# Two-layer diffusion backbone: in each attention unit, the foreign piece behind the scores, then the turn, then the values

## Chip, core and metric

The kernel runs on one core of a Trainium2 chip. The metric is the device time of one execution in microseconds (us), the median of several runs. Five engines work side by side, each through its own queue of instructions in a fixed order: PE (TensorE, matrix products and transposes), DVE (VectorE), ACT (ScalarE), POOL (GpSimd) and SP (SyncE, which here only issues DMAs). PEld is the load of a product's stationary operand, which overlaps PE.

## What is computed

The reference is a backbone of two layers on 128 context tokens and 512 latent tokens, width 1024, in float32. The layer the change touches is the second, attention with 8 query heads and 2 key heads of 128 channels:

```
def blocked_attention(q, k, v):
    ...
    def one_block(qi):
        s = jnp.einsum('bqkgd,bskd->bkgqs', qi, k, ...) * sm_scale
        p = jax.nn.softmax(s, axis=-1).astype(v.dtype)
        return jnp.einsum('bkgqs,bskd->bqkgd', p, v)
...
y = blocked_attention(q, k, v) @ w_o[i]
x = x + g1 * y
```

Latent queries attend to 128 cached and 512 own keys (640 in all), context queries to the 128 context keys. A projection to q, k and v goes before, an output projection behind, and a SwiGLU feed-forward block follows in each layer.

## The kernel before

Every float32 operand of a product is held as two rounded parts, h (high) and l (low), and each product is done three times (h by h, l by h, h by l; the table THREE). The helper `pair` makes the parts: ACT copies the source to h (line 146), a second engine subtracts h from the source to give l (line 147). That engine is DVE, except for the split of weight tiles within the attention loop, where `ws.eng = G` gives it to POOL.

The attention loop runs over 34 units: 32 latent units, named by head and query block (0_0, 0_1, ... 7_3), and two context units, c0 and c1. A unit has these steps:

- `scores`: 6 products into the PSUM tile s_0_0 and so on (3 pairs of 128x320). There is one buffer for it (`ps_tile(..., 0)`), so the next scores wait until this unit's exponentials are read out of it.
- `peak` on DVE (maximum, line 1331, and its scaling, line 1332), `exps` on ACT (line 1338), `weights` (reciprocal, line 1348, then the normalising of pe: on ACT at line 1240 for even query blocks, on DVE at line 1238 for odd ones).
- `turn`: 5 transposes of pe on PE into the one buffer of tile t (`ps_tile(..., 1)`, line 1354). `keep`: `pair` from t to pt_0h and pt_0l, ACT then DVE. The next turn needs that buffer free.
- `values`: for each two query blocks, 15 products (line 1371) from pt into the tile o; `store`: `pair` from o to the attention output, ah and al.

Between them PE is given pieces of other work through `fills`: first `pq`, the q projection of heads 3 to 7 (8 pieces of 6 products each per head, tiles pq_7 to pq_11), then `wa`, the first half of the output projection (4 pieces of 6 products for each of 8 column blocks, wa_0 to wa_7). All of these share the third buffer (`ps_tile(..., 2)`). When a block's last piece is done, its tile is read out: a q head by `scaled` (DVE line 538, ACT lines 543 and 1184), then squares, rotary terms and `pair`; an output block by `residual`, two DVE instructions (lines 513 and 527). Only then may the next block's first product write that buffer. Behind the loop follow the second half of the output projection (wb) and the feed-forward block.

How many pieces go into a unit is decided by the counters `spent` and `work`. A scheduler then fixes the order of each engine's queue from the written order and from its own view of what is ready, so that steps of one unit may stand among those of the next.

Of the kernel before, what the change touches and what calls it, by code (L numbers as in the profile page):

```python
# [62 lines left out]
def hybrid_step(  # L63
# [707 lines left out]
    with tc.tile_pool(name="pool1", bufs=1) as p1:  # L771
# [317 lines left out]
        with tc.tile_pool(name="pool4", bufs=1) as p4:  # L1089
# [11 lines left out]
                last=last0,  # L1101
# [7 lines left out]
    with tc.tile_pool(name="pool2", bufs=1) as p2:  # L1109
# [274 lines left out]
        units = []  # L1384
# [30 lines left out]
        with ExitStack():  # L1415
            for u, unit in enumerate(units):
                pipe.now += 1
                for f in posts:
                    f()
                posts = []  # L1420
                unit.scores()
                last = units[u - 2] if u > 1 and units[u - 2].values else None
                if last:
                    last.values()
                if u:
                    units[u - 1].turn()
                unit.peak()
                unit.exps()
                if u:
                    units[u - 1].keep()  # L1430
                unit.weights()
                spent += W_UNIT + (W_VALUES if last else 0)
                while fills and not posts and spent + W_PIECE / 2 <= work * (u + 1) / len(units):
                    posts = [f for f in (fills.pop(0)(),) if f]
                    spent += W_PIECE
                if last:
                    last.store()
                pipe.run_due()
# [38 lines left out]
    def last1(kn):  # L1477
# [60 lines left out]
        last=last1,  # L1538
# [116 lines left out]
```

## Time and profile before

| what | value |
|---|---|
| median of 3 runs | 1357.52 us (1357.14 to 1358.26) |
| the profiled execution | 1356.08 us, its span 1354.3 us |
| mean granted TensorE clock | 0.993 |
| PE busy | 1326.0 us, 98% of the span |
| DVE, ACT, POOL busy | 1068.6, 637.7, 46.3 us |
| attention loop, first scores to the first product of wb | 709.85 to 867.95 us |

A line of a timeline gives the start, the duration, the engine, the source line, the operation, the tile written and those read, and in brackets how long the engine stood idle before and what ended it. In such lines buffer and unit numbers are left out: `t<-kc,pe` is a turn, whichever unit's. PE starts the next product while the last still drains, so the distance between starts is what a product costs PE; ends lie somewhat later.

### The profile page before, as it was taken

The numbers are of one execution on the slowest core, as the hardware profiler recorded it, in microseconds if no ns is written. First come the engines' busy times: TensorE is split into PE (matmuls) and PEld (weight loads), VectorE is DVE, ScalarE is ACT, GpSimd is POOL, SyncE is SP. The second block draws the span as 40 slices with busy tenths as digits, with TensorE's granted clock in tenths as the row PEclk, the third lists the DMA queues.
The fourth block names the chain that finished last, engine by engine and source line by source line (L and its number), as shares of the span: only waits on it lengthen the run. The fifth ranks groups of instructions, "written<-read, shape, count | busy, mean of one in ns | idle before, by whom it ended". The sixth has DMA issues, their size and how long they took to land.

```text
span 1354.3 us, 22409 instructions
## 1 busy us (share of the span) xinstructions
PE 1326.0 (98%) x8952; PEld 1295.1 (96%) x8952; DVE 1068.6 (79%) x2025; ACT 637.7 (47%) x1159; POOL 46.3 (3%) x56
## 2 busy tenths in 40 slices
PE   8999999999999999999999999999999999999996
PEld 6899999999999999999998999999999999999995
DVE  4899897978999999899877677589876777446744
ACT  5433246753145522454666675477541355314543
POOL 0000000000000000000022221000000000000001
PEclk9999999999999999999999999999999999999998
DMA  9735522125543454334331110131134022311212
GB/s 365 286 125 171 171 94 94 63 67 176 179 141 109 146 187 151 120 137 164 133 101 48 48 48 32 51 137 60 38 137 171 32 94 76 112 63 63 78 47 78
DMA packets 36807, 155.53 MB, mean 115 GB/s; under 512 B 3936, under 2 KB 11104, under 8 KB 25952
## 3 DMA queue, kind: packets, MB, share of 16 engines
q1 hardware_dynamic: 36704, 154.12, 33.0%
q8 instruction: 70, 1.15, 0.4%
q14 instruction: 33, 0.27, 0.1%
HBM read 148.60 MB, written 2.88 MB: 112 GB/s over the span
## 4 chain that ended last, share of the span: by engine, by line
PE 82%; DVE 12%; ACT 3%; issue 2%; DMA 1%; SPq 0%; POOL 0%; DVEq 0%; ACTq 0%; POOLq 0%
PE fi L648 28%; PE fo L294 18%; PE fi L294 8%; PE pi L294 6%; PE pq L294 5%; PE po L294 4%; DVE junk L377 4%; PE wb L294 2%; PE wa L294 2%; PE o L1371 2%; PE s L1321 2%; DVE wl_fi_p L147 1%; PE t L1354 1%; DMA rawa<-wada 1%; DMA x<-xT 1%
## 5 line engine op out<-in xcount | busy, mean ns | idle before, releaser
L146 ACT ACTIVATE wh_fi_p<-raw_fi 128x512 fp32r<-128x512 f32 x252 | 154.5, 627 | 226.0 <-PE fi L648 122.3
L377 DVE CUSTOM_DVE_ANT_0 junk<-rawa,silb 128x512 f32<-128x512 f32 (+1 forms) x280 | 224.0, 800 | 7.9 <-DMA rawa<-wada 3.5
L147 DVE TENSOR_TENSOR wl_fi_p<-raw_fi,wh_fi_p 128x512 fp32r<-128x512 f32 x252 | 171.3, 687 | 65.6 <-ACT wh_fi_p L146 65.3
L146 ACT ACTIVATE wh_fo<-raw_fo 128x1024 fp32r<-128x1024 f32 (+1 forms) x48 | 47.5, 990 | 147.8 <-PE fo L294 129.5
L648 PE MATMUL fi<-bh,wl_fi_p 128*128 128x320 f32 x288 | 89.0, 309 | 0.0
L648 PE MATMUL fi<-bh,wh_fi_p 128*128 128x320 f32 x288 | 88.8, 308 | 0.0
L648 PE MATMUL fi<-ah,wl_fi_p 128*128 128x320 f32 x288 | 88.7, 308 | 0.0
L648 PE MATMUL fi<-al,wh_fi_p 128*128 128x320 f32 x288 | 88.7, 308 | 0.0
L648 PE MATMUL fi<-ah,wh_fi_p 128*128 128x320 f32 x288 | 88.4, 307 | 0.0
L648 PE MATMUL fi<-bl,wh_fi_p 128*128 128x320 f32 x288 | 88.4, 307 | 0.0
L294 PE MATMUL fo<-al,wh_fo 128*128 128x384 f32 (+1 forms) x352 | 81.0, 311 | 0.0
L294 PE MATMUL fo<-ah,wh_fo 128*128 128x384 f32 x352 | 80.8, 311 | 0.1
L294 PE MATMUL fo<-ah,wl_fo 128*128 128x384 f32 x352 | 80.5, 310 | 0.0
L294 PE MATMUL fo<-bh,wh_fo 128*128 128x384 f32 x328 | 75.2, 310 | 0.0
L294 PE MATMUL fo<-bh,wl_fo 128*128 128x384 f32 (+1 forms) x328 | 75.1, 310 | 0.0
L294 PE MATMUL fo<-bl,wh_fo 128*128 128x384 f32 x328 | 75.0, 310 | 0.0
L513 DVE SCALAR_TENSOR_TENSOR x<-fo,mod,x 128x128 f32<-128x128 f32 (+1 forms) x52 | 18.5, 359 | 70.7 <-PE fo L294 67.2
L648 PE MATMUL fi<-x0h,wh_fi_p 128*128 128x320 f32 x216 | 68.1, 319 | 0.5
L648 PE MATMUL fi<-xh,wh_fi_p 128*128 128x320 f32 x216 | 67.9, 320 | 0.5 <-ACT fi L660 0.4
L648 PE MATMUL fi<-xl,wh_fi_p 128*128 128x320 f32 x216 | 66.5, 309 | 0.0
L648 PE MATMUL fi<-xh,wl_fi_p 128*128 128x320 f32 x216 | 66.5, 309 | 0.0
L648 PE MATMUL fi<-x0h,wl_fi_p 128*128 128x320 f32 x216 | 66.4, 308 | 0.0
(376 smaller groups left out, 3774.7 us busy)
## 6 DMA issues: line engine op xcount, KB each, us to landing
raw_fi<-wfi SPq DMA_DIRECT2D x44, 1024.0 KB, 4.8
rawa<-wada SPq DMA_DIRECT2D x84, 512.0 KB, 3.4
raw_fo<-wfo SPq DMA_DIRECT2D x16, 1024.0 KB, 4.9
raw_ada<-wada SPq DMA_DIRECT2D x12, 512.0 KB, 7.3
raw_in<-win SPq DMA_DIRECT2D x6, 1024.0 KB, 5.2
raw_fo<-wfo SPq DMA_DIRECT2D x8, 768.0 KB, 4.3
raw_qkv<-wqkv SPq DMA_DIRECT2D x6, 1024.0 KB, 5.5
raw_out<-wout SPq DMA_DIRECT2D x4, 1024.0 KB, 5.9
```

Of the source, the lines that this page charges most:

```text
L146: S.activation(h, src, AF.Copy)
L147: eng.tensor_tensor(out=l, in0=src, in1=h.bitcast(F32), op=ALU.subtract)
L294: PE.matmul(ps[:, h, 0 : hi - lo], w[a][:, k, cols], rhs[b][:, k0 + k, lo:hi], start=k == 0 and a == b, stop=k == kn - 1 and a == 1,)
L377: op = V.tensor_tensor_reduce(out=self.junk, in0=raw[:, cols], in1=self.silb[:, c, cols], scale=1.0, scalar=0.0, op0=ALU.mult, op1=ALU.add ...
L513: V.scalar_tensor_tensor(out=xs, in0=got[:, 0 : b - a], scalar=mod[l][:, gate0 + m, c : c + 1], in1=xs, op0=ALU.mult, op1=ALU.add,)
L648: PE.matmul(out, w[a][:, k, :], ops.get(OPERAND[p], b)[:, k, :], start=fresh and k == 0 and a == b, stop=k == ops.kn - 1 and a == 1, skip_ ...
L1321: PE.matmul(self.ps[:, hf, 0:HT], bufB[a][:, self.h, q0 : q0 + P], kt[b][:, self.kv, hf * HT : hf * HT + HT], start=n == 0, stop=n == 2,)
L1354: PE.transpose(flat(pt)[:, s * P : s * P + P], self.pe[:, s * P : s * P + P], ident)
L1371: PE.matmul(po[:, 0 : 2 * P], vt[a][:, self.kv, s * P : s * P + P], got[b][:, s, :], start=s == 0 and n == 0, stop=s == 4 and n == 2,)
```

## The change

Within a unit, the written order was scores, values of the unit before last, turn of the last unit, peak, exponentials, keep, weights, pieces, store. It becomes scores, peak, exponentials, pieces, turn and keep of the last unit, values, weights, store. Nothing is added or left out. PE, DVE and ACT run the same instructions in another order within the attention loop; the orders of POOL and of SP's DMAs stay as they were.

```
--- before.py
+++ after.py
@@ -1420,19 +1420,18 @@
                 posts = []
                 unit.scores()
                 last = units[u - 2] if u > 1 and units[u - 2].values else None
-                if last:
-                    last.values()
-                if u:
-                    units[u - 1].turn()
                 unit.peak()
                 unit.exps()
-                if u:
-                    units[u - 1].keep()
-                unit.weights()
                 spent += W_UNIT + (W_VALUES if last else 0)
                 while fills and not posts and spent + W_PIECE / 2 <= work * (u + 1) / len(units):
                     posts = [f for f in (fills.pop(0)(),) if f]
                     spent += W_PIECE
+                if u:
+                    units[u - 1].turn()
+                    units[u - 1].keep()
+                if last:
+                    last.values()
+                unit.weights()
                 if last:
                     last.store()
                 pipe.run_due()
```

Three places show what the scheduler makes of it. Names carry the unit here.

First place, PE queue between the output blocks wa_2 and wa_3 (from the sixth head on). Before, the last two rows of wa_2 and what follows, up to the first rows of wa_3:

```order
L294 MATMUL wa_2_8414<-ah_68,wl_wo0_1_8192 128x384
L294 MATMUL wa_2_8414<-ah_68,wl_wo0_1_8192 128x256
L1321 MATMUL s_5_3_8466<-kth_6548,ah_68 128x320 x2
L1321 MATMUL s_5_3_8466<-ktl_6549,ah_68 128x320 x2
L1321 MATMUL s_5_3_8466<-kth_6548,al_69 128x320 x2
L1371 MATMUL o_5_1_8473<-pt_5_0h_8404,vth_6552 128x256
L1371 MATMUL o_5_1_8473<-pt_5_0l_8405,vth_6552 128x256
...
L1371 MATMUL o_5_1_8473<-pt_5_0h_8404,vtl_6553 128x256
L1354 MATMUL t_5_2_8489<-kc_73,pe_5_2_8445 128x128 x5
L294 MATMUL wa_3_8507<-ah_68,wh_wo0_1_8191 128x384
L294 MATMUL wa_3_8507<-ah_68,wh_wo0_1_8191 128x256
```

Now:

```order
L294 MATMUL wa_2_8386<-ah_68,wl_wo0_1_8164 128x384
L294 MATMUL wa_2_8386<-ah_68,wl_wo0_1_8164 128x256
L1354 MATMUL t_5_1_8454<-kc_73,pe_5_1_8379 128x128 x5
L294 MATMUL wa_3_8479<-ah_68,wh_wo0_1_8163 128x384
L294 MATMUL wa_3_8479<-ah_68,wh_wo0_1_8163 128x256
L1321 MATMUL s_5_3_8466<-kth_6548,ah_68 128x320 x2
L1321 MATMUL s_5_3_8466<-ktl_6549,ah_68 128x320 x2
L1321 MATMUL s_5_3_8466<-kth_6548,al_69 128x320 x2
```

Before, scores (s_5_3), 15 products of values (o_5_1) and a turn (t_5_2) lay between the end of wa_2 and the start of wa_3. Now only a turn (t_5_1) does. The same holds from wa_1 to wa_2, wa_3 to wa_4 and wa_4 to wa_5.

The same place in DVE's queue, before:

```order
L1331 TENSOR_REDUCE mx_5_2_8442<-s_5_2_8429 128x1
L1332 TENSOR_SCALAR mx_5_2_8442<-mx_5_2_8442,rq_6554 128x1
L147 TENSOR_TENSOR pt_5_0l_8405<-t_5_1_8436,pt_5_0h_8404 128x5x128
L1348 RECIPROCAL su_5_2_8446<-su_5_2_8446 128x1
L513 SCALAR_TENSOR_TENSOR x_67<-wa_2_8414,mod1_78,x_67 128x128
L527 SCALAR_TENSOR_TENSOR x_67<-wa_2_8414,mod1_78,x_67 128x512
L1331 TENSOR_REDUCE mx_5_3_8495<-s_5_3_8466 128x1
L1332 TENSOR_SCALAR mx_5_3_8495<-mx_5_3_8495,rq_6554 128x1
```

Now:

```order
L1331 TENSOR_REDUCE mx_5_2_8436<-s_5_2_8429 128x1
L513 SCALAR_TENSOR_TENSOR x_67<-wa_2_8386,mod1_78,x_67 128x128
L1332 TENSOR_SCALAR mx_5_2_8436<-mx_5_2_8436,rq_6554 128x1
L527 SCALAR_TENSOR_TENSOR x_67<-wa_2_8386,mod1_78,x_67 128x512
L1348 RECIPROCAL su_5_2_8440<-su_5_2_8440 128x1
L147 TENSOR_TENSOR pt_5_0l_8406<-t_5_1_8454,pt_5_0h_8405 128x5x128
L1331 TENSOR_REDUCE mx_5_3_8473<-s_5_3_8466 128x1
L1332 TENSOR_SCALAR mx_5_3_8473<-mx_5_3_8473,rq_6554 128x1
```

The two read-outs of wa_2 (lines 513 and 527) moved ahead of the keep of t_5_1, and the first of them stands between the maximum of unit 5_2 and its scaling.

Second place, PE queue about the turn of unit 1_1 (the pq phase), before:

```order
L294 MATMUL pq_8_7352<-bh_70,wh_qkv4_0_7181 128x322
L1354 MATMUL t_1_1_7497<-kc_73,pe_1_1_7468 128x128 x5
L294 MATMUL pq_8_7352<-bl_71,wh_qkv4_0_7181 128x320
L294 MATMUL pq_8_7352<-bl_71,wh_qkv4_0_7181 128x322
L294 MATMUL pq_8_7352<-bh_70,wl_qkv4_0_7182 128x320
L294 MATMUL pq_8_7352<-bh_70,wl_qkv4_0_7182 128x322
L1371 MATMUL o_1_1_7531<-pt_1_0h_7471,vth_6552 128x256
L1371 MATMUL o_1_1_7531<-pt_1_0l_7472,vth_6552 128x256
L1371 MATMUL o_1_1_7531<-pt_1_0h_7471,vtl_6553 128x256
```

Now:

```order
L294 MATMUL pq_8_7324<-bh_70,wl_qkv4_0_7180 128x322
L1354 MATMUL t_1_1_7509<-kc_73,pe_1_1_7446 128x128 x5
L1371 MATMUL o_1_1_7570<-pt_1_0h_7461,vth_6552 128x256
L1371 MATMUL o_1_1_7570<-pt_1_0l_7462,vth_6552 128x256
L1321 MATMUL s_1_3_7524<-kth_6548,ah_68 128x320 x2
L1321 MATMUL s_1_3_7524<-ktl_6549,ah_68 128x320 x2
L1321 MATMUL s_1_3_7524<-kth_6548,al_69 128x320 x2
L1371 MATMUL o_1_1_7570<-pt_1_0h_7461,vtl_6553 128x256
L294 MATMUL pq_9_7541<-bh_70,wh_qkv4_1_7318 128x320
```

Before, four products of pq_8 stood behind the turn, and eight of the values ahead of the scores s_1_3. Now the first values stand directly behind the turn, and the scores behind the second of them. The same shape stands at the turns of 0_1 (seven values, then the scores), 2_1 and 3_3.

Third place, ACT's queue about the turns of head 0, before:

```order
L146 ACTIVATE pt_0_0h_7241<-t_0_0_7229 128x5x128
L1338 ACTIVATE pe_0_1_7238,su_0_1_7239<-s_0_1_7222,mx_0_1_7235,rq_6554 128x640
L146 ACTIVATE pt_0_0h_7241<-t_0_1_7272 128x5x128
L146 ACTIVATE wh_qkv5_0_7565<-raw_qkv5_6912 128x1024
L146 ACTIVATE ah_68<-q_2_7152 128x640
L1338 ACTIVATE pe_0_2_7281,su_0_2_7282<-s_0_2_7265,mx_0_2_7278,rq_6554 128x640
```

Now:

```order
L1338 ACTIVATE pe_0_1_7232,su_0_1_7233<-s_0_1_7222,mx_0_1_7229,rq_6554 128x640
L146 ACTIVATE pt_0_0h_7259<-t_0_0_7253 128x5x128
L146 ACTIVATE wh_qkv5_0_7537<-raw_qkv5_6912 128x1024
L146 ACTIVATE pt_0_0h_7259<-t_0_1_7290 128x5x128
L146 ACTIVATE ah_68<-q_2_7152 128x640
L1338 ACTIVATE pe_0_2_7275,su_0_2_7276<-s_0_2_7265,mx_0_2_7272,rq_6554 128x640
```

The split of a weight tile (wh_qkv5_0), whose second half POOL does, stood behind the copy of t_0_1 and stands ahead of it now. On DVE, as before, the rotary sum of head 2 and the scaling of unit 0_2's maximum stand ahead of the subtraction for t_0_1.

## The prediction

> **What bounds the kernel now.** The first section of the page gives the bound, and the table of stretches the place. The stretches run from the scores of 0_1 (716.84) over those of 1_1, 2_1, 3_0 and 4_3 and those of 7_0 to the first product of wb (867.95).
>
> ```profile
> PE 1326.0 (98%) x8952; PEld 1295.1 (96%) x8952; DVE 1068.6 (79%) x2025; ACT 637.7 (47%) x1159; POOL 46.3 (3%) x56
> ...
> core 0: us, PE busy (x) PEld busy (x) DVE busy (x) ACT busy (x) POOL busy (x), PEclk, DMA share, GB/s
> ...
> 716.84:736.42 19.58, 17.89 (x122) 16.51 (x123) 13.71 (x27) 12.70 (x24) 3.70 (x2) 1.00 0.10 25
> 736.42:755.92 19.50, 18.32 (x135) 17.55 (x134) 13.23 (x29) 12.75 (x26) 3.83 (x3) 1.00 0.22 68
> 755.92:776.03 20.11, 19.60 (x146) 18.89 (x146) 14.17 (x31) 12.81 (x31) 4.49 (x3) 1.00 0.06 14
> 776.03:807.67 31.64, 30.67 (x224) 29.44 (x224) 24.33 (x56) 23.44 (x49) 6.96 (x4) 1.00 0.16 49
> 807.67:849.62 41.95, 41.95 (x313) 41.44 (x313) 30.41 (x66) 23.41 (x47) 6.08 (x3) 1.00 0.08 28
> 849.62:867.95 18.33, 17.64 (x126) 16.77 (x125) 12.33 (x27) 10.58 (x23) 0.00 (x0) 1.00 0.17 59
> ```
>
> PE is the bound with 98%. In these six stretches it stands idle 1.69, 1.18, 0.51, 0.97, 0.00 and 0.69 us, 5.04 in all: no reordering of the loop can win more, and all but the last 0.69 lies in the four stretches with pq pieces. The wa stretch, 41.95 us long, has no idle time to win, only some to lose. What PE waited for in the loop:
>
> ```profile
> engine line waited for: us in total, times, longest us
> PE t L1354 <- DVE pt_0l L147: 1.3, 3, 0.6
> PE o L1371 <- DVE pt_0l L147: 1.2, 2, 0.7
> PE t L1354 <- DVE pt_2l L147: 1.0, 1, 1.0
> PE t L1354 <- ACT pe L1240: 0.7, 1, 0.7
> PE o L1371 <- ACT pt_0h L146: 0.6, 3, 0.2
> ```
>
> Every wait hangs on a turn: on the turned weights being kept (ACT, then DVE), or on the normalised weights before it. None is for a piece's buffer. One such place, the turn of 1_1 and what follows, in the timeline:
>
> ```profile
> 742.42 0.77 PE L1354 MATMUL t<-kc,pe 128*128 128x128 f32 x5 [0.48 <-DVE pt_0l L147]
> ...
> 743.22 0.70 ACT L146 ACTIVATE pt_0h<-t 128x640 fp32r<-128x640 f32 x1 [1.32 <-PE t L1354]
> ...
> 743.82 1.05 ACT L146 ACTIVATE wh_qkv<-raw_qkv 128x1024 fp32r<-128x1024 f32 x1
> ...
> 743.99 0.81 DVE L147 TENSOR_TENSOR pt_0l<-t,pt_0h 128x640 fp32r<-128x640 f32 x1
> ...
> 744.76 0.88 ACT L1338 ACTIVATE pe<-s,mx,rq 128x640 f32<-128x640 f32 x1
> ...
> 744.86 0.39 PE L1371 MATMUL o<-pt_0l,vth 128*128 128x256 f32 x1 [0.50 <-DVE pt_0l L147]
> ...
> 745.79 0.41 PE L1321 MATMUL s<-kth,ah 128*128 128x320 f32 x1
> ```
>
> From the turn's start it is 0.80 to the copy, 1.57 to the subtraction, 2.44 to the values that need the low part. The next scores come 1.03 behind the start of the exponentials. I call a turn's cost to PE 0.46 (five starts), a product of values 0.12, a piece's product 0.15.
>
> **The change, part by part.** No instruction is added, so the sum is of waits that go and waits that come.
>
> *Handing over the pieces' buffer (wa_1 to wa_2, 2 to 3, 3 to 4, 4 to 5).* A block's buffer is free when both instructions of `residual` are done:
>
> ```profile
> 806.34 0.46 PE L294 MATMUL wa<-ah,wl_wo 128*128 128x384 f32 x2
> ...
> 806.84 0.35 DVE L513 SCALAR_TENSOR_TENSOR x<-wa,mod,x 128x128 f32<-128x128 f32 x1 [0.38 <-PE wa L294]
> 807.10 0.74 DVE L527 SCALAR_TENSOR_TENSOR x<-wa,mod,x 128x512 f32<-128x512 f32 x1
> ...
> 823.98 0.46 PE L294 MATMUL wa<-ah,wl_wo 128*128 128x384 f32 x2
> ...
> 824.74 0.74 DVE L527 SCALAR_TENSOR_TENSOR x<-wa,mod,x 128x512 f32<-128x512 f32 x1
> ...
> 827.55 0.54 PE L294 MATMUL wa<-ah,wh_wo 128*128 128x384 f32 x2
> ```
>
> The last products of a block end at 806.80, the read-out at 807.84: 1.04 later, with DVE idle before it. From DVE's end to PE's start is another 0.06 (743.99 + 0.81 to 744.86). Before the change this cost nothing, since scores, 15 values and a turn cover it: one block ends at 824.44, its read-out at 825.48, and the next block starts only at 827.55, with 2.07 to spare. That cover goes. Only the turn is left, whose 0.46 starts about 0.16 before the last product's end, so it covers 0.30. PE idles 1.04 + 0.06 - 0.30 = 0.80 at the first of the four places. At the other three, DVE's queue has the scaling of the next maximum between the two read-outs, about 0.13 more: 0.93. The first product after a wait takes 0.54 instead of 0.46, 0.08 each time. Sum: 0.80 + 3 x 0.93 + 4 x 0.08 = 3.9 us. Some tenths go at the scores of this stretch, which no longer start just behind their exponentials; I take 3.8. The bounds: 2.9 (the read-out 0.25 quicker at each place) and 4.4 (each held up by another DVE instruction of about a tenth). The scaling also waits for the piece there, so the exponentials of 5_2 come about 1.1 late, but the scores behind them are released at about the moment at which the two wa_3 products end, so this adds nothing more.
>
> *Turn, values and scores without a piece between (second place of the change).* At 1_1 the copy follows the turn's start by 0.80, and the exponentials the copy by 0.60 now (before by 1.54, with the weight split between them). Scores could start at 0.80 + 0.60 + 1.03 = 2.43; the second value product starts at 2.44 and the scores at 2.56. PE's work in this time is 0.46 + 2 x 0.12 = 0.70, so it idles 1.86. Before, the span was 3.37 (742.42 to 745.79) with 0.46 + 4 x 0.15 + 8 x 0.12 = 2.02 of work: 1.35 idle. So 0.5 more here; the turn itself, late by 0.48 before, is some 0.1 to 0.2 earlier in its order. I take +0.4 for this head, the same for head 2 (four context products partly fill it), and +0.7 for head 3, where the turn of 3_3 now has one value product and then the scores: 0.46 + 0.12 of work in some 2.5 us, 1.9 idle, against this wait before, which it replaces:
>
> ```profile
> 792.38 1.55 DVE L1238 TENSOR_SCALAR pe<-pe,su 128x640 f32<-128x640 f32 x1
> ...
> 795.05 0.76 PE L1354 MATMUL t<-kc,pe 128*128 128x128 f32 x5 [0.97 <-DVE pt_2l L147]
> ```
>
> Together +1.5, between 0.2 (the present idle time moved, not raised) and 2.6.
>
> *Head 0 and POOL.* One DVE instruction here took almost three times as long as its like:
>
> ```profile
> 724.08 2.40 POOL L147 TENSOR_TENSOR wl_qkv<-raw_qkv,wh_qkv 128x1024 fp32r<-128x1024 f32 x1 [3.46 <-ACT wh_qkv L146]
> ...
> 724.79 2.37 DVE L147 TENSOR_TENSOR al<-q,ah 128x640 fp32r<-128x640 f32 x1
> 727.09 0.15 DVE L1348 RECIPROCAL su<-su 128x1 f32<-128x1 f32 x1
> ...
> 728.16 0.77 PE L1354 MATMUL t<-kc,pe 128*128 128x128 f32 x5 [0.69 <-ACT pe L1240]
> ...
> 742.28 0.81 DVE L147 TENSOR_TENSOR al<-q,ah 128x640 fp32r<-128x640 f32 x1
> ```
>
> It ended 0.68 behind POOL's split (726.48) and cost PE the 0.69 at 728.16. The Trainium skill (SBUF — State Buffer, "Who interferes with whom") says that a VectorE instruction with two SBUF inputs and a GpSimd instruction that reads SBUF shut each other out for a whole instruction, and that one that reads PSUM is not held; by that rule the trace agrees, 2.37 against 0.81. Now ACT's half of this split stands ahead of the copy for t_0_1, so POOL starts about 0.2 us before that turn. On DVE the rotary product of head 2 meets its start, then the maximum, then the rotary sum (two SBUF inputs) and only then the subtraction for t_0_1. If the rotary product gets in just ahead, POOL ends about 2.7 behind the turn's start, the sum at 3.3, the subtraction at 4.2; six values then bring the scores of 0_3 at 5.05. PE's work there is 0.46 + 7 x 0.12 = 1.30, so it idles 3.75. What goes is the idle of this place now, about 1.6, and the 0.69 with its restart. Sum +1.2, with -0.3 (no meeting) and +1.9 (POOL first) as its ends.
>
> *End of the loop.* The turn of 7_1 waits 0.58 now:
>
> ```profile
> 860.36 0.74 PE L1354 MATMUL t<-kc,pe 128*128 128x128 f32 x5 [0.58 <-DVE pt_0l L147]
> ```
>
> Six more products of wa_7 and the scores of 7_3 change places with it. I take -0.5 of this stretch's 0.69, between -0.7 and +0.2.
>
> **Sum:** 3.8 + 1.5 + 1.2 - 0.5 = +6.0 us. The profiled execution, 1356.08, becomes 1362.1. The median shown, 1357.52, lies 1.44 above it, and what is forecast is a median: 1363.5.
>
> **The rivals.**
>
> *Faster: the pieces cover the turns.* Each of the five rows of waits goes, because a piece now stands ahead of every turn, and the buffer is handed over while PE is at the turn. For it: all present waits hang on turns. That is 4.8 off (the sum of those rows), 1352.7. It decides if a hand-over costs less than about 0.3 at PE; against it stands the 1.10 just worked out, with 0.30 of cover.
>
> *No difference.* Hand-overs at half their price (1.9), heads 1 to 3 at +0.5, head 0 at -0.3, end -0.5: +1.6, 1359.1. For it: each place's waits are also slack for what follows, and DVE has a quarter of the wa stretch idle. Against: PE had none there.
>
> *No meeting at head 0.* All else as forecast: 6.0 - 1.5 = +4.5, 1362.0. The two instructions start within about 0.1 us of each other by my count, so this is close to even.
>
> *The clock falls.* With a wait of almost 4 us, PE's clock could drop. The only rows with less than full clock stand at the end, where PE runs out of work:
>
> ```profile
> 1338.00:1342.00 4.00, 2.52 (x20) 2.19 (x18) 1.90 (x6) 2.53 (x6) 0.00 (x0) 1.00 0.00 0
> 1342.00:1346.00 4.00, 1.14 (x2) 0.42 (x2) 4.00 (x5) 1.82 (x4) 0.00 (x0) 0.61 0.15 55
> 1346.00:1350.00 4.00, 0.00 (x0) 0.00 (x0) 3.47 (x6) 0.00 (x0) 0.00 (x0) 0.50 1.02 361
> ```
>
> At 1.48 idle of 4 it is 1.00; at 2.86 idle of the next 4 it is 0.61, then 0.50. If the wait at head 0 did this for 4 us at 0.50, PE would lose 2 us: 1365.5. The Trainium skill (TensorE: Matmul & The Clock Gate, "What's actually happening") puts the drop behind a whole idle window of about 3.4 us that runs on its own, not from the last product. By that rule a wait of 3.75 with a single product in it seldom fills one.
>
> **How the numbers follow.** The forecast has 0.45, no meeting 0.28, the clock 0.07, no difference 0.15, faster 0.05. The bounds of the terms added up give -0.3 + 0.2 + 2.9 - 0.7 = +2.1 and 1.9 + 2.6 + 4.4 + 0.2 = +9.1, but not all fall on one side: the range from 1359.9 to 1366.0 holds the first three cases and a little of the fourth. A measurement of this kernel tells 0.2%, 2.7 us, from no change. Above 1360.2 is slower: 0.80 (the first three). Same 0.15, faster 0.05.
>
> **What would show it.** Hand-overs: waits of PE for `x` of line 527 at products of wa, about 0.9 each, four times, where there are none now, and the wa stretch 3 to 4.4 us longer. Turns: the idle times before line 1354 mostly gone, those before `o` larger (above 1.5 us in all per head 0 to 2, and one at 3_3 for the scores). Head 0: an `L1142` of 1 to 2 us on DVE beside POOL's 2.40. The forecast is wrong if products of wa show no wait, or if the stretches with pq come out shorter than the 90.83 us that they sum to now.

## The result and the profile after

The changed kernel takes 1367.24 us (median of 6 runs, 1365.98 to 1367.56) against 1357.58 for the one before in the same runs: +9.66 us, ratio 1.007, interval 1.006 to 1.008. Its profiled execution took 1367.51, with a span of 1365.7. The direction was right, the size too small: +6.0 was forecast, and the time lies 1.24 us above the range.

The two profiled executions lie 11.4 us apart (spans of 1354.3 and 1365.7). Of this, 9.65 lies in the attention loop: from the first scores to the first product of wb it took 158.10 us before (709.85 to 867.95) and takes 167.75 now (711.65 to 879.40). The other 1.80 lies ahead of the loop, where nothing was changed: there PE ran at half speed from 40.85 to 47.68 in the profile after, and only from 42.41 to 45.82 in the one before (both had another such time of 3.4 us near 80). That the loop's 9.65 equals the difference of the medians is therefore partly chance. The table of the same six stretches, after:

```profile
718.65:738.63 19.98, 17.57 (x123) 16.63 (x123) 12.48 (x27) 13.01 (x24) 5.29 (x3) 1.00 0.09 25
738.63:759.74 21.11, 19.76 (x134) 19.04 (x134) 13.02 (x30) 12.49 (x26) 3.65 (x2) 0.92 0.20 63
759.74:780.12 20.38, 19.50 (x147) 18.89 (x146) 13.64 (x32) 12.97 (x32) 4.17 (x2) 1.00 0.06 14
780.12:815.08 34.96, 31.23 (x225) 29.64 (x224) 25.60 (x57) 23.81 (x49) 6.09 (x3) 1.00 0.14 44
815.08:860.46 45.38, 42.43 (x314) 41.46 (x313) 29.85 (x66) 23.07 (x45) 6.10 (x3) 1.00 0.08 25
860.46:879.40 18.94, 17.64 (x128) 16.79 (x126) 13.70 (x28) 11.95 (x25) 0.00 (x0) 1.00 0.16 57
```

Set against the lengths of before this is +0.40, +1.61, +0.27, +3.32, +3.43 and +0.61. The second stretch has a granted clock of 0.92, which no stretch of before has. What PE waits for in the loop, after:

```profile
PE wa L294 <- DVE x L527: 4.1, 5, 1.2
PE o L1371 <- ACT pt_0h L146: 2.5, 3, 0.9
PE o L1371 <- ACT pt_2h L146: 1.4, 1, 1.4
PE pq L294 <- ACT q L1184: 1.3, 2, 1.0
PE o L1371 <- DVE pt_0l L147: 1.0, 2, 0.5
PE o L1371 <- DVE qsq L1212: 0.9, 1, 0.9
PE s L1321 <- ACT q L543: 0.5, 1, 0.5
PE s L1321 <- ACT pe L1338: 0.4, 1, 0.4
PE o_c L1297 <- DVE pt_c0l L147: 0.2, 1, 0.2
```

All waits at the turn itself (line 1354) are gone. In their place stand five waits for the read-out of an output block and two for that of a q head (the pieces' buffer, 5.4 us in all), and waits of values and scores behind the turns. Two hand-overs, the place about c0 and the turn of 3_3, from the timeline of after:

```profile
822.52 0.46 PE L294 MATMUL wa<-ah,wl_wo 128*128 128x384 f32 x2
...
822.82 0.71 PE L1354 MATMUL t<-kc,pe 128*128 128x128 f32 x5
...
823.29 0.74 DVE L527 SCALAR_TENSOR_TENSOR x<-wa,mod,x 128x512 f32<-128x512 f32 x1
...
824.18 0.53 PE L294 MATMUL wa<-ah,wh_wo 128*128 128x384 f32 x2 [0.65 <-DVE x L527]
...
870.03 0.20 DVE L1332 TENSOR_SCALAR mx<-mx,rq 128x1 f32<-128x1 f32 x1
870.16 0.74 DVE L527 SCALAR_TENSOR_TENSOR x<-wa,mod,x 128x512 f32<-128x512 f32 x1
...
871.05 0.53 PE L294 MATMUL wa<-ah,wh_wo 128*128 128x384 f32 x2 [1.17 <-DVE x L527]
...
783.08 2.39 POOL L147 TENSOR_TENSOR wl_wo<-raw_wo,wh_wo 128x1024 fp32r<-128x1024 f32 x1 [3.80 <-ACT wh_wo L146]
783.15 0.15 DVE L1212 SCALAR_TENSOR_TENSOR qsq<-qms,qsq 128x5 f32<-128x5 f32 x1
...
783.40 2.10 DVE L1213 TENSOR_SCALAR qsq<-qsq 128x5 f32<-128x5 f32 x1
783.45 0.36 PE L1371 MATMUL o<-pt_2h,vth 128*128 128x256 f32 x1 [0.87 <-DVE qsq L1212]
...
785.41 0.81 DVE L538 TENSOR_TENSOR q<-pq,rstd 128x640 f32<-128x640 f32 x1
786.63 0.56 PE L294 MATMUL pq<-bh,wh_qkv 128*128 128x320 f32 x2 [0.35 <-ACT q L1184]
...
804.99 0.38 PE L1371 MATMUL o<-pt_2h,vth 128*128 128x256 f32 x1 [1.42 <-ACT pt_2h L146]
...
805.86 0.56 PE L1321 MATMUL s<-kth,ah 128*128 128x320 f32 x2 [0.48 <-ACT q L543]
```

The other three hand-overs wait 0.77 each. From the end of a block's last product to the end of its read-out it is 1.05 at the first (822.98 to 824.03) and 1.17 at those three, and PE starts 0.15 later at each. The last two lines are what waits behind the turn of 3_3. At c0 the values of 2_3 wait for line 1212, which reads the norm's products (`qms`): `ps_small` has two buffers in turn, and with the turn of c0 now ahead of those values, they get the buffer that the norm holds. Then line 1213, 0.16 us before, takes 2.10 beside POOL's split, and the read-out of pq_10 (line 538) waits behind it.

### The profile page after: what moved, and what is told of

Read it like the earlier page. It is cut to its first block, busy times and chain, and to the rows that moved or that the text cites. A ratio compares the mean times of both kernels' runs of the same rounds, so it can differ in the third digit from the quotient of the medians.

```text
span 1365.7 us, 22412 instructions
## 1 busy us (share of the span) xinstructions
PE 1329.9 (97%) x8952; PEld 1298.4 (95%) x8952; DVE 1068.0 (78%) x2025; ACT 640.1 (47%) x1159; POOL 46.5 (3%) x56
## 4 chain that ended last, share of the span: by engine, by line
PE 79%; DVE 13%; ACT 4%; issue 2%; DMA 2%; SPq 0%; POOL 0%; DVEq 0%; ACTq 0%; POOLq 0%
PE fi L648 28%; PE fo L294 18%; PE fi L294 8%; PE pi L294 6%; PE pq L294 5%; PE po L294 4%; DVE junk L377 4%; PE wb L294 2%; PE s L1321 2%; PE o L1371 1%; PE wa L294 1%; DVE wl_fi_p L147 1%; DMA rawa<-wada 1%; PE t L1354 1%; DMA x<-xT 1%
```

## The experiments

Times and ratios are against the kernel before in the same runs. In several kernels `new` chooses, unit by unit, between the two written orders. "Loop" is the length from the first scores to wb in the trace, 158.10 before and 167.75 after. A slow window is a time of 3.4 us in which PE ran at half speed; the section on the clock says more of it.

**The changed order in the wa part alone.**

```
+new = u >= 19          # the changed order from unit 4_2 on, that of before ahead of it
```

> The changed order only from unit 4_2 on, the order of before in the units ahead of it. Theory A (each place pays by itself, for the hand-overs of the pieces' buffer): the stretches from 4_3 to wb grow as in the changed kernel, 3.43 + 0.61 us, and those ahead stay as before, so +4.0 us, 1361.6. Rival B (the waits of the wa stretch are a queue inherited from the heads ahead, which leave DVE late): without them the wa stretch grows by less than 1.5 us, so 1359 or less.

1361.4 (1359.95 to 1363.05), ratio 1.003 (1.0019 to 1.0041), +3.7. The last three stretches of its trace:

```profile
776.80:807.26 30.46, 30.46 (x225) 29.48 (x224) 22.73 (x55) 23.51 (x49) 7.15 (x4) 1.00 0.16 50
807.26:852.80 45.54, 42.59 (x314) 41.50 (x313) 30.04 (x67) 22.52 (x45) 6.08 (x3) 1.00 0.08 26
852.80:871.80 19.00, 17.69 (x128) 16.87 (x126) 13.76 (x28) 11.94 (x25) 0.00 (x0) 1.00 0.17 56
```

The wa stretch and the end cost what they cost in the changed kernel (+3.59, +0.67), with the same five waits: theory A. The first row is a by-catch. This stretch still has the order of before, yet it takes 30.46 in place of 31.64, without idle time. In the profile of before, POOL's rotary product began just ahead of a DVE instruction (line 1238, which took 1.55), here just behind it. The first line is of before, the next two are of this run, and the last one is of the last run of this section, which also has the order of before in this stretch:

```profile
792.29 1.29 POOL L1141 TENSOR_TENSOR q<-q,ropes 128x512 f32<-128x512 f32 x1 [7.64 <-ACT pe L1338]
...
793.15 0.55 DVE L1238 TENSOR_SCALAR pe<-pe,su 128x640 f32<-128x640 f32 x1
793.35 1.51 POOL L1141 TENSOR_TENSOR q<-q,ropes 128x512 f32<-128x512 f32 x1 [7.94 <-ACT ah L146]
...
794.36 0.77 PE L1354 MATMUL t<-kc,pe 128*128 128x128 f32 x5 [0.89 <-DVE pt_2l L147]
```

So the 0.97 us wait at the turn of 3_3, which the prediction counted as removed, hangs on which of the two engines begins first, and that differs from trace to trace. In the last run POOL is first again, line 1238 takes 1.47 and the turn waits 0.89; here, and where seven units are put back below, DVE is first, line 1238 takes 0.55 and 0.56, and there is no such wait.

**The changed order in the pq part alone.**

```
+new = u < 19
```

> The reverse: the changed order up to unit 4_1, the order of before from 4_2 on. Theory A: the stretches ahead of 4_3 grow as in the changed kernel, 0.40 + 1.61 + 0.27 + 3.32 = 5.6 us with the clock drop of head 1 and about 4.0 without it, those behind stay as before: 1363.1 or 1361.5. Rival B (all is one chain, so a calm end takes back what the heads lost): less than +2, 1359.5 or less.

1363.55 (1362.29 to 1365.09), ratio 1.0044 (1.0031 to 1.0057), +5.9; loop 163.13. With +3.7 this makes 9.6: the two parts add up. The stretches ahead of 4_3 grew by 0.42, 0.10, 0.25 and 3.68, the wa stretch by 0.57. Head 1 has the waits of the changed kernel, at full clock and without its loss:

```profile
740.80:760.40 19.60, 18.24 (x135) 17.53 (x134) 13.03 (x30) 12.50 (x26) 3.64 (x2) 1.00 0.21 68
760.40:780.76 20.36, 19.48 (x147) 18.88 (x146) 13.78 (x32) 12.93 (x32) 4.16 (x2) 1.00 0.06 14
780.76:816.08 35.32, 31.64 (x226) 29.86 (x225) 26.28 (x57) 23.78 (x50) 6.10 (x3) 1.00 0.15 46
```

**A smaller read-out of the output blocks.** It leaves out most of the sum of the first half of the output projection.

```
-xs = halves(x[:, m, CTX:T])
+xs = halves(x[:, m, CTX:T])[:, :, 0:16]     # and the same columns of wa
```

> The changed kernel, with line 527's read-out of the blocks wa_0 to wa_7 cut from 512 to 32 columns (so most of that sum is left out of x). Theory A (PE waits for the read-out of the pieces' buffer): the read-out falls from 1.04 to about 0.6 us behind the last product, of which the turn covers 0.3, so the five waits of 0.65 to 1.17 us fall below 0.3 each, -2.5 to -3.5 us, 1364.2. Rival C (PE waits there because DVE is late altogether, or for the next scores, which would then be waited for instead): less than 1 us is won, 1366.5.

1365.48 (1361.83 to 1368.4), ratio 1.006 (1.0044 to 1.0075). The waits at the blocks fell by 0.5 each (one by 0.65, to nothing; the last is still 0.68):

```profile
829.03 0.53 PE L294 MATMUL wa<-ah,wh_wo 128*128 128x384 f32 x2 [0.27 <-DVE x L540]
...
865.37 0.53 PE L294 MATMUL wa<-ah,wh_wo 128*128 128x384 f32 x2 [0.68 <-DVE x L540]
```

The wa stretch went from 45.38 to 43.59 and the end from 18.94 to 18.39, -2.34: theory A in the trace. The median shows only 1.8 of it; the runs lie 6.6 us apart, which the section on the clock takes up. The median alone does not decide between the two theories, the waits do.

**The pieces moved, turn and values in their old order.**

```
+if last: last.values()
 if u: units[u - 1].turn(); units[u - 1].keep()
-if last: last.values()
```

> One part of the change alone: the pieces directly behind the scores, but the values ahead of the turn as before. Theory A: at the hand-overs wa_2 to 3, wa_4 to 5 and wa_6 to 7 the scores now stand between, so these three waits (0.77, 0.77, 1.17) go, those at wa_1 to 2 and wa_3 to 4 stay; the heads keep their turn with one or no value product ahead of the scores, so their waits stay: -2.7 us against the changed kernel, 1364.5. Rival D (the turn standing ahead of the values is what costs): all of the 9.7 us goes, 1357.5. Rival E (only the pieces' place counts, turn and values do not): 1367.2.

1365.66 (1364.82 to 1368.74), ratio 1.0067 (1.0055 to 1.0079): -1.6 against the changed kernel, less than the -2.7 of theory A and within the intervals of the two ratios. Three hand-overs lost their wait, but the scores that now stand there wait for their exponentials, as at 834.26:

```profile
834.26 0.56 PE L1321 MATMUL s<-kth,ah 128*128 128x320 f32 x2 [0.55 <-ACT pe L1338]
```

**Turn and values swapped, the pieces where they were.**

```
 unit.scores()
-if last: last.values()
 if u: units[u - 1].turn()
+if last: last.values()
```

> The other part of the change alone: the pieces stay at the unit's end as before, the turn (and its keep, as before behind the exponentials) stands ahead of the values. Theory A (what costs is that no piece stands between a turn and what follows it, and at a block's end only a turn): pieces and values still follow each turn, and turns of one pair of query blocks come further apart (27 products between the turns of 1_0 and 1_1, 14 before), so the waits for the turned weights at heads 1 and 2 shrink and no wait for x of line 527 comes: between -1.5 and +0.5 us, 1357.0. Rival D (the turn ahead of the values is the costly part): +3 or more, 1360.7.

1362.96 (1361.81 to 1364.55), ratio 1.0047 (1.0035 to 1.006). Theory A is wrong: at heads 1 and 2 the stretches are 19.40 and 20.36, hardly changed, but near c0 o_c waits 1.32 for pt_c0l, and the stretch from 3_0 is 35.96, with a slow window of the clock (from 786.82) in it. By the medians the pieces alone cost +8.0 and the swap alone +6.5, so the halves do not add up to the whole. They are not alike, though: in the loop PE stands idle 5.2 us before, 12.8 in the changed kernel, 12.6 with the pieces alone and 8.4 with the swap alone. Most of the waits come with the place of the pieces. That one half takes a cover away and the other finds it gone would fit this, but no run shows it.

**The order of before put back about c0.**

```
+new = u not in (12, 13, 14)
```

> The changed kernel, but the order of before in the three units c0, 3_0 and 3_1. Theory A (the four waits of 0.87, 0.35, 0.23 and 0.37 us about c0 come from this place's own order: the turn of 2_3 behind the pieces, the turn of c0 ahead of the values 2_3, which puts those values into the buffer that the norm of head 5 still holds): the stretch from 3_0 to 4_3 loses 1.8 to 2.4 us, 1365.0. Rival B (the waits pass on to the next turn, that of 3_1 or 3_3): less than 0.8 us, 1366.6.

1368.09 (1365.73 to 1368.2), ratio 1.0078 (1.0065 to 1.0091): nothing won. The four waits are gone, and others have come ahead of and behind the place. PE's idle time fell by 0.4 us in the stretch from 3_0 (3.73 to 3.34) and rose by 0.8 in the one ahead (0.88 to 1.69). This trace also has a second slow window, from 804.89, behind the last of these waits, so the length of its stretch from 3_0 (35.42) says little. Three of the waits that came:

```profile
775.13 0.77 PE L1354 MATMUL t<-kc,pe 128*128 128x128 f32 x5 [0.81 <-DVE pt_2l L147]
...
802.46 0.39 PE L1371 MATMUL o<-pt_2h,vth 128*128 128x256 f32 x1 [0.79 <-ACT pt_2h L146]
...
805.08 0.90 PE L1321 MATMUL s<-kth,ah 128*128 128x320 f32 x2 [2.24 <-ACT q L543]
```

**The order of before put back at 4_0 and 4_1.**

```
+new = u not in (17, 18)
```

> The changed kernel, but the order of before in the two units 4_0 and 4_1. Theory A (the waits of 1.42 and 0.48 us behind the turn of 3_3 come from having only one product of values between it and the scores of 4_1, and the split of a weight tile ahead of the copy on ACT): eight products of pq_11 and the values of 3_3 stand behind the turn again, both waits go, -1.5 to -2.2 us with the restarts, 1365.4. Rival B (the split of the weight tile alone holds it, wherever the turn stands, or the wait goes to the next turn): less than 0.7 us, 1366.7.

1365.55 (1363.91 to 1367.56), ratio 1.0066 (1.0053 to 1.008). Its loop takes 166.21 at full clock; the changed kernel's, with head 1 at e2's 19.60, would take 166.24. The waits moved (0.35 and 0.68 in place of 1.42 and 0.48, and one of 0.94 in the stretch behind): rival B.

**The splits on DVE.**

```
-spent, posts, ws.eng = 0, [], G
+spent, posts, ws.eng = 0, [], V
```

> The changed kernel, with the l parts of the weight tiles in the loop made by DVE in place of POOL. Theory P (POOL's splits hold up DVE's instructions with two SBUF inputs: al of head 2, 2.11 for 0.82, and with it the read-out for which pq_8 waits 0.99; line 1213 near c0, 2.10 for 0.17, and with it pq_11's 0.35): these two waits of pq fall below 0.3 each, and no DVE instruction of those forms is over 1.3. Against it stand about ten splits of 1.22 us in DVE's queue, each behind or ahead of a read-out: the sum between -1.5 and +3 us, 1367.5. Rival Q (DVE is late at these places because of its own queue, not POOL's): both waits of pq stay at 0.9 and 0.3 or grow.

1366.76 (1366.64 to 1370.82), ratio 1.0082 (1.0069 to 1.0095). Both waits of pq are gone, line 1213 is back at 0.16, and al of head 2 at 0.83:

```profile
726.15 0.83 DVE L147 TENSOR_TENSOR al<-q,ah 128x640 fp32r<-128x640 f32 x1
...
785.30 0.16 DVE L1213 TENSOR_SCALAR qsq<-qsq 128x5 f32<-128x5 f32 x1
```

Theory P holds for these instructions. The first stretch gains (18.17), but the whole does not (+10.35 by the median). At head 1 the turned weights wait for DVE (1.10 and 0.67), and PE's idle time there rises from 1.35 to 2.56. The profiled execution is the slowest of the five (1370.82) and has four slow windows in the loop, two of them at head 1, so its other stretches are not to be compared by length.

**Idle products behind four turns.**

```
+for s in range(FILL.get(self.nm, 0)):      # 0_1, 1_1, 2_1: 3; 3_3: 6
+    PE.matmul(flat(pt)[:, 640 : 640 + 2 * P], vt[0][...], kt[0][...], start=True, stop=True)
```

> The changed kernel, with idle products of 128x256 behind four turns (3 behind those of 0_1, 1_1 and 2_1, 6 behind that of 3_3), written into the unused columns of the turn's tile and read by nobody. In the traces so far PE's clock fell for a whole window of 3.41 us when the window before it held under about 2460 columns of products, and did not when it held over about 2690 (a full one holds some 7400). Theory K (the count of columns in the window decides): with 768 to 1536 columns more, no window of the attention loop is slow in the trace, though the waits stay; the loop takes 166 to 167 us and the time 1366.0 to 1366.8, against 1367.5 for the executions with a slow window. Rival L (the clock follows the length of the longest wait, or the waits for turned weights as such): slow windows still come at heads 1 or 3, and the time is 1367.5 or more.

1366.5 (1365.31 to 1368.39), ratio 1.007 (1.0058 to 1.0082), loop 167.04, no slow window in the loop. Not decisive: without the extra columns only one window (from 800.43, some 2290 of its 3820 columns) would have been low in this execution, and the timed runs are spread as before.

**The order of before in all seven units from c0 to 4_1.**

```
+new = u not in range(12, 19)
```

> The changed kernel with the order of before in all of the units c0 to 4_1 (seven units; undone for three and for two of them before, the waits turned up again behind the undone units). Theory B (the waits of this stretch pass from turn to turn as long as any part of it has the changed order): now the stretch from 3_0 to 4_3 falls to 30.5 to 31.7 us, from 34.96, with no wait of PE above 1 us in it, so -3.3 to -4.5 us, 1363.3. Rival A (each place pays by itself): the sum of what the two smaller undoings saved in that stretch at full clock, at most 1.6 us, 1365.7.

1363.18 (1361.6 to 1367.77), ratio 1.0053 (1.0039 to 1.0067).

```profile
757.67:779.02 21.35, 19.66 (x146) 18.92 (x146) 15.59 (x34) 14.26 (x33) 3.66 (x2) 1.00 0.06 14
779.02:809.11 30.09, 30.09 (x225) 29.42 (x224) 22.33 (x54) 22.81 (x48) 6.38 (x3) 1.00 0.16 50
```

Theory B: undone as a whole, the stretch falls from 34.96 to 30.09 without idle time, 0.97 of it given back in the stretch ahead. The two smaller undoings did not add up to this, so in this part of the loop the loss belongs to the run of units rather than to the two places. The units 3_2 and 3_3 were put back only here; what they would do alone no run shows.

**An attempt to beat the kernel before:** its order, two splits of head 0 on DVE.

```
+ws.eng = V if u < 5 else G
```

> An attempt to beat the kernel before: its order, with the l parts of the two weight tiles that are split in head 0 (qkv4) made by DVE in place of POOL. With all splits on DVE, the changed kernel's stretch from 0_1 to 1_1 took 18.17 us in place of 19.98, while head 1 lost more. Theory P (POOL's split holding DVE is what head 0 of before waits for, 1.6 us at the turn of 0_1 and the next): the stretch falls from 19.6 to about 18.2 us and the others stay, 1356.0. Rival Q (the splits, 1.22 us each, only move DVE's lateness, and the split of qkv5, which stays on POOL, still meets the rotary products): no change within 0.1%, 1357.4, or up to 1 us slower.

1355.31 (1354.2 to 1356.81) against 1356.95, ratio 0.9987 (0.9978 to 0.9996): 1.6 us faster, the best of all kernels here, though by little more than the interval. The trace shows it in heads 0 and 1 (19.08 and 18.92 for 19.58 and 19.50); the split of qkv5, left on POOL, still holds al for 2.12, so the 18.2 of theory P was not reached. Both splits that moved run ahead of these two stretches (at 703.31 and 709.94), and the same order gave 19.78 at head 1 in the first run of this section, so where the gain comes from stays open.

## The clock

In the changed kernel, behind the turn of 1_1, PE ran at half speed for a while:

```profile
746.37 0.38 PE L1371 MATMUL o<-pt_0h,vth 128*128 128x256 f32 x1 [0.79 <-ACT pt_0h L146]
747.23 0.44 PE L1371 MATMUL o<-pt_0l,vth 128*128 128x256 f32 x1 [0.48 <-DVE pt_0l L147]
747.47 0.73 PE L1321 MATMUL s<-kth,ah 128*128 128x320 f32 x2
...
747.00:747.50 0.50, 0.27 (x2) 0.27 (x3) 0.50 (x2) 0.19 (x2) 0.50 (x1) 0.91 0.00 0
747.50:748.00 0.50, 0.50 (x3) 0.50 (x3) 0.48 (x2) 0.06 (x1) 0.50 (x1) 0.50 0.00 0
...
750.50:751.00 0.50, 0.50 (x4) 0.50 (x3) 0.00 (x0) 0.50 (x1) 0.00 (x0) 0.67 1.08 459
```

Read at 0.05 us, it is at half speed from 747.4 to 750.85, and in the same execution from 40.85 to 47.7 and from 81.8 to 85.25. The falls lie 40.95 and 665.6 us apart: 12 and 195 times 3.413. In all thirteen traces the falls lie on such a grid within 0.05 us, and the grid lies differently in each execution. So the clock holds for whole windows of 3.413 us. What sets it seems to be the work in the window before. The table adds up the columns of the products that ran in that window (320 for a 128x320, shared out by time where a product lies across the edge; a full window holds about 7350, since 642 columns take 0.298). It has every window of the loops of all thirteen traces that ran at full speed and was followed by half speed, and some of the lowest that were followed by full speed:

| window before | columns | next window |
|---|---|---|
| c0 put back, 801.48 | 381 | half speed |
| turn first, 783.41 | 1553 | half speed |
| splits on DVE, 804.21 | 1593 | half speed |
| small read-out, 797.78 | 1621 | half speed |
| values first, 743.93 | 1946 | half speed |
| splits on DVE, 742.77 | 2113 | half speed |
| c0 put back, 743.45 | 2304 | half speed |
| splits on DVE, 766.66 | 2335 | half speed |
| after, 744.00 | 2401 | half speed |
| seven units back, 722.85 and 743.33 | 2452 and 2606 | full speed |
| after, 723.52 and 802.03 | 2715 and 2885 | full speed |
| c0 put back, 722.97 | 2736 | full speed |
| before, 742.14 (its lowest) | 3270 | full speed |

In the loop, a window with less than about a third of its columns was followed by a slow one, with the limit between 2401 and 2452; some records are missing from each trace. The count is not the whole measure: elsewhere in the trace with the splits on DVE, windows with 2884 columns (from 377.54) and 3008 (from 1353.76, near the end) were followed by a slow one too, and in its loop a window that was itself slow (from 746.18) was followed by another at 2625. The limit is read off the traces; the one run that added columns did not put it to the test. The Trainium skill (TensorE: Matmul & The Clock Gate, "What's actually happening") gives a free-running window of 3.413 us, and the traces agree. It puts the fall behind an idle window; here the window was not idle, it held up to 2401 columns in the loop.

One slow window costs 1.5 us (21.11 against 19.60 at head 1). Whether a wait causes one depends on where the grid falls. This would explain the two groups of times of the changed kernel, though only the profiled execution has a trace: 1365.98 and 1366.01 at a mean clock of 0.992, the other four, 1366.97 to 1367.56, at 0.991. The kernel with the small read-out ran from 1361.83 at 0.995 to 1368.4 at 0.989, which may be why its median says less than its trace.

## Why the prediction was right in direction and wrong in size

At full clock the change costs 8.1 us in the loop (9.65 less the 1.5 at head 1), where 6.0 was forecast; the slow window adds 1.5 in the profiled execution. Even the upper bounds of all terms added up, +9.1, lie below the 9.65. Of the 3.6 us above the forecast, head 3 brings 2.6, the slow window 1.5 and the end of the loop 1.1; the other terms came out 1.6 smaller than forecast. By the steps of the sum:

- *Handing over the pieces' buffer, +3.8*: the stretch took +3.43, at the four places named, 0.65 and three times 0.77 where 0.80 and 0.93 were worked out. The two are not counted alike: the profile counts idle time from the turn's end, 0.71 behind its start, the prediction from 0.46 behind it. By the prediction's count PE lost 0.90 and 1.02, because its start came 0.15 behind the read-out and not 0.06. The smaller read-out and the wa part alone show both place and cause. The step missed a fifth such place, wa_6 to wa_7 (1.17), and two for q heads (0.99 and 0.35). It looked only where a turn alone stood between two output blocks.
- *End of the loop, -0.5*: measured +0.61, outside its bounds. The wait of 0.58 at the turn of 7_1 went as forecast, but the fifth hand-over took its place.
- *Heads 1 and 2, +0.4 each*: +0.10 at full clock and +0.27, a little less than forecast.
- *Head 3, +0.7*: the step that failed, measured +3.32; with heads 1 and 2 that is +3.69 at full clock, where 2.6 was the upper bound of the three. The waits behind the turn of 3_3 are 1.42 + 0.48 = 1.90, just as worked out. But the stretch was priced by that one turn. The place about c0, where waits of 1.82 us and POOL's hold on line 1213 came, was not walked through. Nor would its price alone have done: with either place put back by itself, waits came at others, and only the seven units together gave the stretch back. The 0.97 that was counted as won at the turn of 3_3 was no sure gain either, since two of four traces with the order of before do not have it.
- *Head 0, +1.2* (its own figures, 3.75 less 1.6, 0.69 and a restart of 0.08, give +1.4): measured +0.40, inside its bounds, but by another path. The rotary sum (line 1142, 724.73) got in ahead of POOL (724.92), and what was held was the next instruction with two SBUF inputs, al of head 2, for 2.11; it cost the 0.99 at the hand-over of a q head, not a wait of 3.75. The direction of the meeting was a guess at 0.1 us, and was named as that.

```profile
724.73 0.68 DVE L1142 TENSOR_TENSOR q<-q,rs_q 128x512 f32<-128x512 f32 x1
...
724.92 2.73 POOL L147 TENSOR_TENSOR wl_qkv<-raw_qkv,wh_qkv 128x1024 fp32r<-128x1024 f32 x1 [2.65 <-ACT wh_qkv L146]
...
726.21 2.11 DVE L147 TENSOR_TENSOR al<-q,ah 128x640 fp32r<-128x640 f32 x1
```

- *The clock*, a rival with 0.07: it came, at head 1, behind waits of 0.79 and 0.48. The prediction tied it to one long wait and to head 0; by the traces it goes with little work in a window, and short waits are enough.

What stays open is how the loss in the seven units divides between POOL's hold on DVE, the buffer of `ps_small` and the order of ACT's copies: with the splits on DVE line 1213 was free and PE's idle time in the stretch fell from 3.73 to 2.82, but that trace also had a slow window there.

## What to carry to other kernels

Before a piece of filler is moved, list every buffer hand-over on that engine, old and new, with what stands between the last write and the next; each one without cover costs read-out plus release (here 1.20 to 1.32 from the last product's end at four of the five places) less the cover. Price a reordered run of dependent units as a whole: here, waits that vanished at one place turned up at the next. Distrust a wait that rests on two engines meeting within some tenths of a us; it can stand in one execution and be missing from the next.

## What had not been expected of the hardware

Two waits of 0.79 and 0.48 us stood ahead of 3.41 us at half of PE's clock, in a window with 2401 of some 7350 columns; two such waits (0.80 and 0.47), with the changed order in the pq part alone, cost nothing of the kind. A 128x5 `TENSOR_SCALAR` (line 1213) took 2.10 us for 0.16 beside POOL's split.
